# Two matmuls in place of three in the token-half products of a two-layer decoder trunk on one Trainium2 core

## The chip, the cores and the metric

The kernel runs on one core of a Trainium2 chip. The metric is the device time of one execution in microseconds. Three runs of the kernel before gave 1172.56, 1173.91 and 1175.39 us, so its median is 1173.91 us. One further execution was taken by the hardware profiler and took 1172.98 us; every duration quoted below comes from that one execution.

## The reference: what is computed

One sequence of 512 tokens with 1024 features passes through two layers in float32. Each layer is a token mixer, a layer norm over (alpha times the residual plus the mixer's output), a two-matrix feed-forward block of width 4096 with a squared ReLU, and a second layer norm:

```
mix = jnp.concatenate([s5_out, sb_out], axis=-1) @ mix_w_out[i] + mix_b_out[i]   # layer 0
mix = conformer_conv(x, ...)                                                     # layer 1
x = layer_norm(DEEPNORM_ALPHA * x + mix, ln1_g[layer], ln1_b[layer])
ffn = sqrelu_mlp(x, ffn_w1[layer], ffn_b1[layer], ffn_w2[layer], ffn_b2[layer])
x = layer_norm(DEEPNORM_ALPHA * x + ffn, ln2_g[layer], ln2_b[layer])
```

The mixer of layer 0 is a state-space part beside stick-breaking attention; that of layer 1 is a gated projection, a causal depthwise convolution of 31 taps, a layer norm, a swish and a projection.

## The kernel before, in words

Activations lie with features on the 128 partitions and the 512 tokens along the free dimension, in tiles of 128x512. Every operand of a large product is split into a high part (rounded to the matmul's input type) and a low part (the rest). ScalarE writes the high part and VectorE the low one, L246 and L247 for activations, L110 (`whi`) and L111 (`wlo`) for weights. `gemm` (L250) then spends three matmuls for each block of 128 features: high weights by high activations, high weights by low activations, low weights by high activations, all summed in one PSUM bank (L256). Each of the three loads its own 128x128 weights into TensorE.

**Tails.** Three products are followed by a layer norm and are therefore done in two token halves of 256 columns each, by the class `Tail` (L1004): tail "a", the attention half of layer 0's mixer output (4 feature blocks `cat[4:8]`, PSUM tiles `tla`); tail "b", the last feed-forward block of layer 0 (8 hidden blocks `hs`, tiles `tlb`); tail "d", the last projection of layer 1's convolution module (8 blocks `cs`, tiles `tld`). Each has 8 output tiles per half, 16 in all. When one is complete, VectorE adds it to the residual tile X (L389 with a bias in tails a and b, L385 without one in tail d), and adds X into a running sum over the 8 tiles (`sa`, `sb`, `sd`, L385).

**Layer norm and lead.** `tail_norm_lead` (L1058) sets the order. The first token half of the tail comes first. Then the norm of that half is interleaved with products of the second half: a matmul with a matrix of ones averages the running sum over the features (`mpa` and so on, L954), VectorE subtracts the mean from the 8 X tiles, ScalarE squares them, VectorE adds the squares in pairs, eight more matmuls average them (`vpa`), ScalarE and three small VectorE operations form the reciprocal square root (`ra`, `ta`), and for each of the 8 tiles VectorE scales X, ScalarE writes the new high part (`xah`) and VectorE the new low part (`xal`, L994). `BEFORE = (1, 3, 1, 2)` says how many products at least stand ahead of each averaging matmul. The next product, "lead" (class `Lead`, tiles `fl` and `pl`), uses the normed half at once, and while it works on the first half of the tokens the second half is normed.

**Order of the work.** A planner (the Tile framework's list scheduler) turns the traced instructions into one fixed queue per engine. Among instructions that its own cost model holds ready, it takes the one that was traced first. Each engine then works through its queue in order. In the convolution stage, TensorE, VectorE and ScalarE are kept in the order of `CONV_ORDER` by explicit dependencies (`in_order`); the first three products of tail d (the entries "t") lie inside that order. Weights are fetched and split ahead of use (`Weights._prep`, L85): when a tail in layer 0 asks for its weights, up to 5 further units are split too, and these are traced ahead of the tail's additions.

**Buffers.** Split activations lie in a pool of 24 pages of 128x512 (`page`, L208), and half of the hidden activations of the feed-forward blocks of layer 0 in 16 somewhat longer pages (`hpage`, L877), which the convolution uses later. Output tiles lie in 6 PSUM banks (`nps`, L871).

Of the kernel before, what the change touches and what calls it, by code (L numbers as in the profile page):

```python
# [10 lines left out]
F32R = mybir.dt.float32r  # L11
I32 = mybir.dt.int32
AF = mybir.ActivationFunctionType
ALU = mybir.AluOpType
PSUM = bass.MemoryType.PSUM

P = 128
T = 512
H = 256
D = 1024  # L20
KT = D // P
# [171 lines left out]
        self.run.append(ins.name)  # L193


@with_exitstack
def kernel(ctx: ExitStack, tc: tile.TileContext, a: dict, out: bass.AP):
    nc = tc.nc
# [6 lines left out]
    def const(shape, name, dt=F32):  # L205
        return cst.tile(shape, dt, tag=name, name=name)

    def page(name, dt=F32R):  # L208
        return pgp.tile([P, T], dt, tag="pg", name=name, bufs=24)

    X = [const([P, T], f"X{j}") for j in range(KT)]
    ident = const([P, P], "ident")
# [32 lines left out]
    def split(hi, lo, src):  # L245
        i0 = S.copy(hi, src).ins  # L246
        i1 = V.tensor_sub(lo, src, hi.bitcast(F32)).ins  # L247
        return i0.name, i1.name

    def gemm(ps, w, ksl, xs, c0, c1, start=True, stop=True):  # L250
# [6 lines left out]
                                stop=stop and k == n - 1 and i == 2).ins  # L257
        return ins


    wst = ExitStack()
    wpool = wst.enter_context(tc.tile_pool(name="mw", bufs=1))
# [68 lines left out]
    xs, w0, u0 = [], None, mm("u0")  # L331
# [11 lines left out]
    for j in range(KT):  # L343
        ps = (mm if j % 2 else s5ps)(f"xT{j}")
        for b in range(4):
            ins = PE.transpose(ps[:, b * P : (b + 1) * P], xin[j][:, b, :], ident).ins
            if j == 0 or j > 2:
                tc.add_manual_dep(ins, u0_last.name, NOSYNC, reason="order of the first products")
        xh, xl = page(f"x0h{j}"), page(f"x0l{j}")
# [6 lines left out]
        xs.append((xh, xl))  # L356
# [27 lines left out]
    def tt(o, x, y, op):  # L384
        V.tensor_tensor(o, x, y, op=op)  # L385
        return o

    def stt(o, x, s, y, op0, op1):
        V.scalar_tensor_tensor(o, x, s, y, op0=op0, op1=op1)  # L389
        return o  # L390
# [290 lines left out]
    def attention(p):  # L681
# [74 lines left out]
                              start=summed[h] == 1, stop=summed[h] == 4, skip_group_check=True)  # L756

        def closed(_):
            ch, cl = page(f"ch{p}"), page(f"cl{p}")
            split(ch, cl, made["av"])  # L760
            cat[4 + p] = (ch, cl)

        return {"t": turned, "s": scores, "w": weigh, "v": values, "e": closed}

# [5 lines left out]
    def gelu(q):  # L770
        g1 = spage(f"g1{q}")
        act(g1, vv[q], AF.Square)
        ts(g1, g1, GELU_A, 1.0, ALU.mult, ALU.add)
        tt(g1, g1, vv[q], ALU.mult)
        act(g1, g1, AF.Tanh, scale=GELU_C)
        stt(g1, g1, 1.0, vv[q], ALU.add, ALU.mult)
        for t in range(4):
            nc.sync.dma_start(Yd[q].rearrange("(r f) (t c) -> t f r c", r=4, t=4)[t], g1[32 * t : 32 * t + 32])
        yf = att.tile([P, T], F32, tag="wt", name=f"yf{q}", bufs=MIX_BUFS[4])
        nc.sync.dma_start(yf, Yd[q])  # L780
        yh, yl = page(f"yh{q}"), page(f"yl{q}")
        act(yh, yf, AF.Copy, scale=0.5)
        stt(yl, yf, 0.5, yh.bitcast(F32), ALU.mult, ALU.subtract)
        ys.append((yh, yl))

    glu_ws = []

    def glu(m):
        if m % 2 == 0:
            glu_ws[:] = W.next(), W.next()  # L790
        wv, wg = glu_ws
        sl = slice(m % 2 * P, (m % 2 + 1) * P)
        pg_, pv_ = mm(f"gg{m}"), mm(f"gv{m}")
        gemm(pg_, wg, sl, ys, 0, T)
        gemm(pv_, wv, sl, ys, 0, T)
        sg = spage(f"sg{m}").rearrange("p r c -> p (r c)")
# [4 lines left out]
        ch, cl = page(f"gh{m}"), page(f"gl{m}")  # L801
        split(ch, cl, o)
        cat[m] = (ch, cl)


    mo_w = []
# [56 lines left out]
    wp2 = wst.enter_context(tc.tile_pool(name="w2", bufs=1))  # L863
    hst = ExitStack()
    hid = hst.enter_context(tc.tile_pool(name="hid", bufs=1, side="right"))
    nps_ = ctx.enter_context(tc.tile_pool(name="nps", bufs=6, space=PSUM))
    sps_ = ctx.enter_context(tc.tile_pool(name="stp", bufs=2, space=PSUM))
    HALVES = ((0, H), (H, T))
# [5 lines left out]
    def stp(name):  # L874
        return sps_.tile([P, T], F32, tag="st", name=name)

    def hpage(name, dt=F32R, w=T):  # L877
        return hid.tile([P, PAD + T + 2], dt, tag="hid", name=name, bufs=16)[:, :w]
# [125 lines left out]
    class Tail:  # L1004
# [67 lines left out]
    def ffn1(layer, bi, k0, nb, xs, fps, first=()):  # L1072
        hs = []
        for i in range(nb):
            m = k0 + i
            if i < len(first):
                ps = first[i]
            else:
                ps = fps(f"f{layer}{m}")
                gemm(ps, W.next(), slice(0, P), xs, 0, T)  # L1080
            r = tmp(f"fr{layer}{m}")
            act(r, ps, AF.Relu, bias=pv("ffn_b1", 32 * layer + m))
            tt(r, r, r, ALU.mult)
            pg_ = page if (i < 4) == (bi % 2 == 0) else hpage
            hh, hl = pg_(f"hh{layer}{m}"), pg_(f"hl{layer}{m}")
            split(hh, hl, r)
            hs.append((hh, hl))
# [27 lines left out]
    for bi, nb in enumerate(FFN_BLOCKS[0]):  # L1115
# [390 lines left out]
```

## Time and profile before

| | before |
|---|---|
| median of three runs | 1173.91 us |
| profiled execution | 1172.98 us |
| its span (first to last instruction) | 1171.2 us |
| outside the span | 1.8 us |
| TensorE busy | 1138.9 us, 97% |
| VectorE busy | 822.9 us, 70% |
| ScalarE busy | 551.7 us, 47% |
| granted TensorE clock, mean | 0.993 |

PE is TensorE's matmul side, PEld its weight loads, DVE VectorE, ACT ScalarE. In a timeline each row has the start, the time until the last of its instructions ended, the engine, the line, the tiles as out<-in, the shape, how many instructions the row merges, and in brackets the idle time of the engine before it with what ended it. The last instructions of a merged row overlap: a row's time divided by its count is longer than the distance from start to start for short rows. In a table by stretches, each engine has its busy time and instruction count. Sums of times below are taken against the profiled execution of 1172.98 us.

### The profile page before, as it was taken

The page shows a single profiled execution, that of the slowest core. Times are in us where ns is not written, and L with a number is a line of the kernel's source. Part 1 is how long each engine was busy: PE and PEld are TensorE (multiplying, and loading weights), DVE is VectorE, ACT ScalarE, POOL GpSimd, SP SyncE. Part 2 cuts the span into 40 slices and gives each one's busy share as a digit, 9 for nine tenths or more (in the row PEclk, how much of TensorE's full clock was granted, in tenths as well). Part 3 has the DMA queues.
Part 4 walks back from the last instruction along what each step waited for, and adds up shares of the span by engine and source line. Part 5 has one row for each costly group of instructions (what it writes and reads, how often), then busy time and mean ns, then how long its engine had stood idle before and what let it go on. Part 6 is the DMA issues. An engine that isn't in the chain of part 4 may idle for free.

```text
span 1171.2 us, 17896 instructions
## 1 busy us (share of the span) xinstructions
PE 1138.9 (97%) x7180; PEld 953.1 (81%) x7180; DVE 822.9 (70%) x1396; ACT 551.7 (47%) x838; POOL 67.0 (6%) x125
## 2 busy tenths in 40 slices
PE   9989999999999999999999999899989999999997
PEld 7777767799888888888999777599968888887885
DVE  7999875498646546546555899886785958587337
ACT  7857779345425425425323132662753536363530
POOL 1022210000000000000021110001000000000000
PEclk9999999999999999999999999999989999999999
DMA  8521221332688788788454742206324151514211
GB/s 216 165 56 50 79 85 46 110 116 73 221 286 289 250 287 290 249 286 286 164 177 152 247 144 74 75 9 209 91 79 138 56 151 37 170 36 153 63 55 72
DMA packets 145907, 169.59 MB, mean 145 GB/s; under 512 B 13922, under 2 KB 119138, under 8 KB 145824
## 3 DMA queue, kind: packets, MB, share of 16 engines
q1 hardware_dynamic: 137024, 136.96, 36.7%
q0 software_dynamic: 8640, 31.46, 7.9%
q8 instruction: 56, 0.92, 0.3%
q14 instruction: 27, 0.22, 0.1%
q10 hardware_dynamic: 160, 0.03, 0.0%
HBM read 132.12 MB, written 35.65 MB: 143 GB/s over the span
## 4 chain that ended last, share of the span: by engine, by line
PE 82%; DVE 9%; ACT 4%; issue 2%; DMA 2%; POOL 0%; SPq 0%; DVEq 0%; ACTq 0%; POOLq 0%
PE f L256 24%; PE acf L256 11%; PE s L1390 8%; PE fl L256 5%; PE tlb L256 4%; PE tld L256 4%; PE h L1436 4%; PE pv L256 3%; PE pg L256 3%; PE cw L1165 3%; PE tla L256 2%; PE acmo L256 2%; PE pl L256 2%; DVE wlo L111 1%; PE gg L256 1%
## 5 line engine op out<-in xcount | busy, mean ns | idle before, releaser
L110 ACT CAST whi<-raw 128x1024 fp32r<-128x1024 f32 (+1 forms) x150 | 156.7, 1061 | 257.9 <-PE acf L256 61.0
L111 DVE TENSOR_TENSOR wlo<-raw,whi 128x1024 fp32r<-128x1024 f32 (+1 forms) x150 | 183.8, 1238 | 123.9 <-ACT whi L110 120.5
L256 PE MATMUL f<-xdh,whi 128*128 128x512 f32 x208 | 81.0, 390 | 1.0 <-ACT whi L110 1.0
L256 PE MATMUL f<-xah,whi 128*128 128x512 f32 x208 | 81.1, 390 | 0.0
L256 PE MATMUL f<-xal,whi 128*128 128x512 f32 x208 | 80.9, 389 | 0.0
L256 PE MATMUL f<-xah,wlo 128*128 128x512 f32 x208 | 80.9, 389 | 0.0
L256 PE MATMUL f<-xdl,whi 128*128 128x512 f32 x208 | 80.9, 389 | 0.0
L256 PE MATMUL f<-xdh,wlo 128*128 128x512 f32 x208 | 80.9, 389 | 0.0
L256 PE MATMUL acf<-hh,whi 128*128 128x512 f32 x192 | 75.4, 392 | 0.0
L256 PE MATMUL acf<-hh,wlo 128*128 128x512 f32 x192 | 75.2, 392 | 0.0
L256 PE MATMUL acf<-hl,whi 128*128 128x512 f32 x192 | 74.8, 390 | 0.0
L1390 PE MATMUL s<-whi,ah 128*128 128x512 f32 x168 | 66.0, 400 | 3.3 <-ACT whi L110 2.5
L1390 PE MATMUL s<-wlo,ah 128*128 128x512 f32 x168 | 66.4, 402 | 2.3 <-DVE wlo L111 2.3
L1390 PE MATMUL s<-whi,al 128*128 128x512 f32 x168 | 66.0, 396 | 0.0
L111 DVE TENSOR_TENSOR wlo<-quad,whi 128x1536 fp32r<-128x1536 f32 x28 | 49.0, 1754 | 4.7 <-ACT whi L110 4.4
L110 ACT CAST whi<-quad 128x1536 fp32r<-128x1536 f32 x28 | 41.0, 1478 | 21.9 <-PE f L256 8.0
L389 DVE SCALAR_TENSOR_TENSOR cy<-hp,wdw,cy 128x512 f32<-128x512 f32 (+1 forms) x75 | 49.5, 660 | 0.2 <-ACT cy L185 0.2
L95 POOL DMA_DIRECT2D whi<-kepth x30 | 16.1, 536 | 547.7 <-PE tlb L256 385.5
L256 PEld LDWEIGHTS f<-xdh,whi 128*128 128x128 f32 x208 | 39.0, 188 | 9.4 <-ACT whi L110 1.4
L256 PEld LDWEIGHTS f<-xah,whi 128*128 128x128 f32 x208 | 39.0, 188 | 8.2
L256 PEld LDWEIGHTS f<-xdh,wlo 128*128 128x128 f32 x208 | 39.0, 188 | 8.2
L256 PEld LDWEIGHTS f<-xah,wlo 128*128 128x128 f32 x208 | 39.0, 188 | 8.1
(649 smaller groups left out, 3069.1 us busy)
## 6 DMA issues: line engine op xcount, KB each, us to landing
raw<-in_ffn_w_dram SPq DMA_DIRECT2D x35, 1024.0 KB, 5.6
kepth<-whi SPq DMA_DIRECT2D x30, 512.0 KB, 3.4
keptl<-wlo SPq DMA_DIRECT2D x30, 512.0 KB, 9.4
whi<-kepth POOLq DMA_DIRECT2D x30, 512.0 KB, 3.6
wlo<-keptl POOLq DMA_DIRECT2D x30, 512.0 KB, 4.6
raw<-in_ffn_w_dram SPq DMA_DIRECT2D x28, 512.0 KB, 4.1
raw<-in_conv_w_pw_dram SPq DMA_DIRECT2D x12, 1024.0 KB, 7.3
quad<-in_ffn_w_dram SPq DMA_DIRECT2D x16, 768.0 KB, 4.8
```

What stands on the lines that cost most here:

```text
L95: nc.gpsimd.dma_start(x, d)
L110: i0 = nc.scalar.copy(hi, raw).ins
L111: i1 = nc.vector.tensor_sub(lo, raw, hi.bitcast(F32)).ins
L256: ins = PE.matmul(ps[:, c0:c1], u[:, k, ksl], v[:, c0:c1], start=start and k == 0 and i == 0, stop=stop and k == n - 1 and i == 2).ins
L389: V.scalar_tensor_tensor(o, x, s, y, op0=op0, op1=op1)
L1165: PE.matmul(cps[j, c0][g][C, :], Ds[j][t // 16][R, t % 16, :], hps[j][R, t + c0 : t + c1], start=t < 4, stop=t >= n - 4, tile_position=(R. ...
L1390: PE.matmul(ps, u, v[:, p, :], start=chain == i and p == 0 and n_ == 0, stop=p == len(As) - 1 and n_ == 2, skip_group_check=True)
L1436: PE.matmul(ps, u, v, start=k == 0 and i == 0, stop=k == nb_last - 1 and i == 2)
```

## The change

For the tails alone, `gemm` gives way to `side_by_side`. The high and low parts of one activation block now lie side by side in one tile of 128x2x512 (a `Twin`). One matmul takes the high weights once and streams 256 columns of the high and 256 columns of the low part, 512 in all, into a whole PSUM bank; a second matmul takes the low weights and streams the 256 columns of the high part into the bank's first half. The bank's second half therefore holds high weights by low activations, and VectorE adds it to X with an operation of its own ahead of the one that was there. All other products keep `gemm`. So that the parts lie side by side, the page pool becomes 12 tiles of two pages; single pages are handed out as halves of such a tile. The 16 longer pages are replaced, in the feed-forward stage, by 8 tiles of two pages in a pool of their own, and the longer pages open in its place when tail b has been traced.

```diff
+class Twin(tuple):
+    def __new__(cls, t):
+        self = super().__new__(cls, (t[:, 0, :T], t[:, 1, :T]))
+        self.both = t[:, :, :T]
+        return self
...
+    spare = []
+    def twin(name):
+        return Twin(pgp.tile([P, 2, T], F32R, tag="pg", name=name, bufs=12))
     def page(name, dt=F32R):
-        return pgp.tile([P, T], dt, tag="pg", name=name, bufs=24)
+        if not spare:
+            t_ = pgp.tile([P, 2, T], dt, tag="pg", name=name, bufs=12)
+            spare[:] = t_[:, 1], t_[:, 0]
+        return spare.pop()
...
+    def side_by_side(ps, w, ksl, xs, c0, c1):
+        for k, x in enumerate(xs):
+            PE.matmul(ps, w[0][:, k, ksl], x.both[:, :, c0:c1], start=k == 0, stop=k == len(xs) - 1, skip_group_check=True)
+            ins = PE.matmul(ps[:, :H], w[1][:, k, ksl], x[0][:, c0:c1], start=False, stop=k == len(xs) - 1, skip_group_check=True).ins
+        return ins
...
+    hst2 = ExitStack()
+    htw = hst2.enter_context(tc.tile_pool(name="htw", bufs=1, side="right"))
+    hpg = []
...
     def new_x(name):
-        return [(page(f"{name}h{j}"), page(f"{name}l{j}")) for j in range(KT)]
+        return [twin(f"{name}{j}") for j in range(KT)]
...
-                last = gemm(ps, self.ws[j // nj], slice((j % nj) * P, (j % nj + 1) * P), self.xk, c0, c1)
+                last = side_by_side(ps, self.ws[j // nj], slice((j % nj) * P, (j % nj + 1) * P), self.xk, c0, c1)
                 x = X[j][:, c0:c1]
+                tt(x, ps[:, H:], x, ALU.add)
                 if self.bias is None:
-                    tt(x, ps[:, c0:c1], x, ALU.add)
+                    tt(x, ps[:, :H], x, ALU.add)
                 else:
-                    stt(x, ps[:, c0:c1], self.bias[:, j : j + 1], x, ALU.add, ALU.add)
+                    stt(x, ps[:, :H], self.bias[:, j : j + 1], x, ALU.add, ALU.add)
...
     xs, first = tail_norm_lead(hs, "b", rb[1], ("ln2_g", 0), ("ln2_b", 0), 4, "pl")
+    hst2.close()
+    hpg.append(hst.enter_context(tc.tile_pool(name="hpg", bufs=1, side="right", reuse_waits="tile")))
```

The other places of the diff only build twins where two pages stood (x0, y, g, c, the hidden tiles).

More of the change, by code (lines that the diff above doesn't have):

```diff
@@ L348 @@
                 tc.add_manual_dep(ins, u0_last.name, NOSYNC, reason="order of the first products")
-        xh, xl = page(f"x0h{j}"), page(f"x0l{j}")
+        xh, xl = x0 = twin(f"x0{j}")
         with tc.high_priority():
@@ L355 @@
         S.copy(X[j], ps)
-        xs.append((xh, xl))
+        xs.append(x0)
         if j > 1:
@@ L758, in closed @@
         def closed(_):
-            ch, cl = page(f"ch{p}"), page(f"cl{p}")
-            split(ch, cl, made["av"])
-            cat[4 + p] = (ch, cl)
+            cat[4 + p] = twin(f"c{p}")
+            split(*cat[4 + p], made["av"])
         return {"t": turned, "s": scores, "w": weigh, "v": values, "e": closed}
@@ L780, in gelu @@
         nc.sync.dma_start(yf, Yd[q])
-        yh, yl = page(f"yh{q}"), page(f"yl{q}")
+        yh, yl = y = twin(f"y{q}")
         act(yh, yf, AF.Copy, scale=0.5)
         stt(yl, yf, 0.5, yh.bitcast(F32), ALU.mult, ALU.subtract)
-        ys.append((yh, yl))
+        ys.append(y)
     glu_ws = []
@@ L800, in glu @@
         V.tensor_copy(o.rearrange("p (c t) -> p t c", t=4), sg.rearrange("p (t c) -> p t c", t=4))
-        ch, cl = page(f"gh{m}"), page(f"gl{m}")
-        split(ch, cl, o)
-        cat[m] = (ch, cl)
+        cat[m] = twin(f"g{m}")
+        split(*cat[m], o)
     mo_w = []
@@ L875, in stp, with htwin @@
         return sps_.tile([P, T], F32, tag="st", name=name)
+    def htwin(name):
+        return Twin(htw.tile([P, 2, T], F32R, tag="hid", name=name, bufs=8))
     def hpage(name, dt=F32R, w=T):
-        return hid.tile([P, PAD + T + 2], dt, tag="hid", name=name, bufs=16)[:, :w]
+        return hpg[0].tile([P, PAD + T + 2], dt, tag="hid", name=name, bufs=16)[:, :w]
     def tmp(name, dt=F32):
@@ L1083, in ffn1 @@
             tt(r, r, r, ALU.mult)
[L1084 to L1087, printed above, removed]
+            hs.append((twin if (i < 4) == (bi % 2 == 0) else htwin)(f"h{layer}{m}"))
+            split(*hs[-1], r)
             for k in keep_at.get(("f", m), ()) if layer == 0 else ():
```

## The prediction, as put on record

> **What bounds the kernel now.** I read the page's busy times first, then the chain of work that ended last.
>
> ```profile
> span 1171.2 us, 17896 instructions
> PE 1138.9 (97%) x7180; PEld 953.1 (81%) x7180; DVE 822.9 (70%) x1396; ACT 551.7 (47%) x838; POOL 67.0 (6%) x125
> PE 82%; DVE 9%; ACT 4%; issue 2%; DMA 2%; POOL 0%; SPq 0%; DVEq 0%; ACTq 0%; POOLq 0%
> ```
>
> TensorE is the bound overall. But a mean of 70% for VectorE says nothing about a stage, so I asked for busy times by stretches, with the end of tail a and its norm in the first four and tails b and d in the last two:
>
> ```profile
> 234.00:240.00 6.00, 5.93 (x49) 5.96 (x50) 5.47 (x7) 2.84 (x3) 0.00 (x0) 1.00 0.56 171
> 240.00:250.00 10.00, 10.00 (x83) 9.85 (x82) 9.32 (x21) 3.18 (x4) 0.00 (x0) 1.00 0.76 240
> 250.00:260.00 10.00, 10.00 (x79) 9.79 (x79) 9.84 (x26) 4.59 (x13) 0.00 (x0) 1.00 0.02 5
> 260.00:267.00 7.00, 7.00 (x60) 7.00 (x60) 6.36 (x17) 2.32 (x5) 0.00 (x0) 1.00 0.00 0
> ...
> 566.00:619.00 53.00, 53.00 (x417) 51.66 (x416) 31.28 (x67) 13.16 (x25) 7.57 (x14) 1.00 0.48 163
> 758.00:811.00 53.00, 52.85 (x420) 50.86 (x417) 41.81 (x112) 26.45 (x58) 6.34 (x12) 1.00 0.36 120
> ```
>
> Columns after the length are PE, PEld, DVE, ACT, POOL. In tail a TensorE and VectorE are both full: 9.84 of 10 us at 250 to 260. In tail b VectorE is busy 31.28 of 53 us, in tail d 41.81 of 53. The same change meets three different stages.
>
> **What TensorE saves.** Counts are from the views of the tiles, pitches from the chain in order of time, where a run of like matmuls is one row:
>
> ```profile
> L256 PE MATMUL tla<-ch,whi x64: 278/283/466, 234.1 to 259.1; 128*128 128x256 f32 x64
> L256 PE MATMUL tlb<-hh,whi x128: 277/283/471, 571.0 to 618.7; 128*128 128x256 f32 x128
> L256 PE MATMUL tld<-csh,whi x128: 279/283/467, 758.1 to 810.2; 128*128 128x256 f32 x128
> ```
> ```profile
> 439.91 43.52 PE f L256 x192
> ...
> 788.86 8.63 PE tld L256 x72
> ```
>
> 512 columns take 43.52/192 = 226.7 ns from start to start, 256 columns 8.63/72 = 119.9 ns. The 256 further columns cost 106.8 ns, so each matmul carries 13.1 ns that do not depend on its columns. Three matmuls of 256 are 359.7 ns, one of 512 plus one of 256 is 346.6: 13.1 ns saved per block and output tile. That is 64 x 13.1 = 0.84 us in tail a and 128 x 13.1 = 1.68 us each in tails b and d, 4.2 us in all. No row shows a matmul whose moving columns come in two pieces, or the two widths alternating. Bounds: nothing saved, or all fixed parts hidden (39.3 ns, 12.6 us); I take 13.1 ns, since both widths pay the same fixed part in these rows. The Trainium skill ("TensorE: Matmul & The Clock Gate", section Back-to-back issue gap) gives N/2.4 + 2.5 ns, thus a fixed part of only 2.5 ns; the rows show five times that. By the Trainium skill's page, as an estimate, the three tails together would save 0.8 us, and the sum below would be +3.6 us instead.
>
> **What VectorE pays.** 16 additions per tail, 48 in all, of the form in tail d's row:
>
> ```profile
> L385 DVE TENSOR_TENSOR X<-tld,X x16: 409/420/426, 763.5 to 810.8; 128x256 f32<-128x256 f32 x16
> ```
>
> Queued behind an independent instruction, such an operation moves the queue by less than its duration. Tail a's VectorE timeline:
>
> ```profile
> 237.21 0.48 DVE L389 SCALAR_TENSOR_TENSOR X<-tla,rb,X 128x256 f32<-128x256 f32 x1 [0.53 <-PE tla L256]
> 237.61 2.35 DVE L111 TENSOR_TENSOR wlo<-raw,whi 128x1024 fp32r<-128x1024 f32 x2
> ...
> 246.70 0.88 DVE L385 TENSOR_TENSOR sa<-sa,X 128x256 f32<-128x256 f32 x2
> ...
> 248.36 1.75 DVE L385 TENSOR_TENSOR X<-X,mpa 128x256 f32<-128x256 f32 x5 [0.40 <-PE mpa L954]
> ...
> 255.60 0.42 DVE L389 SCALAR_TENSOR_TENSOR ta<-vpa,ra 128x256 f32<-128x256 f32 x1
> ...
> 257.66 1.27 DVE L389 SCALAR_TENSOR_TENSOR X<-X,PV,ra 128x256 f32<-128x256 f32 x3
> ...
> 267.54 2.74 DVE L385 TENSOR_TENSOR X<-X,mpa 128x256 f32<-128x256 f32 x8 [1.14 <-PE mpa L954]
> ```
>
> Five independent ones take 1.75 us: (1.75 - 0.42)/4 = 0.33 us each. Two of which the second needs the first take 0.88: 0.46 us. The new addition and the old one write the same X, so 0.46 holds unless the planner puts something between them. Bounds 0.33 and 0.46; I take 0.33, because in a full stage the planner has other work to put between.
>
> *Tail a.* Before the first mean come 8 new additions, 2.7 us, of which the 0.53 us idle ahead of 237.21 takes part: the mean is 2.1 us late. The ninth tile's addition fits the 0.40 us of idle at 248.36. Those of tiles 10 to 12 are traced ahead of `ta`, another 1.0 us. So the first new high part is D = 3.1 us late. What waits is TensorE's lead:
>
> ```profile
> 258.18 1.32 ACT L185 ACTIVATE xah<-X,PV 128x256 fp32r<-128x256 f32 x3 [2.71 <-DVE X L389]
> ```
> ```profile
> 259.46 0.40 PE L256 MATMUL fl<-xah,whi 128*128 128x256 f32 x2
> ```
> ```profile
> 276.00 0.56 PE L256 MATMUL fl<-xah,whi 128*128 128x256 f32 x3
> 276.59 0.39 PE L256 MATMUL fl<-xal,whi 128*128 128x256 f32 x1
> ```
>
> The first high part is there at 258.18 + 0.5 = 258.7, the lead starts at 259.46: 0.8 us of slack. With D = 3.1 the lead starts 2.3 us late, although the tail's matmuls end 0.84 us earlier. For the second half, tiles 13 to 16 add 1.3 us, so its norm is 4.4 us late in all. There the slack is some 0.2 us: TensorE has run out of first-half products by 276.00, where it picks up the second half's first high parts and then waits 0.3 us. So tail a ends in a loss of 4.4 - 0.2 = 4.2 us; its saving of 0.84 is spent as waiting. Bounds: -0.84 us (all hidden) and 16 x 0.46 - 0.53 - 0.2 = +6.6 us. From there on the stage is TensorE's again: 165 x 0.1199 = 19.8 us of matmuls fill 20.17 us, so the loss stays.
>
> ```profile
> 276.59 20.17 PE fl L256 x165
> ```
>
> *Tail b.* The additions hide: TensorE's places for the averaging matmuls are set by the products ahead of them, not by VectorE.
>
> ```profile
> 600.24 1.43 DVE L385 TENSOR_TENSOR sqb<-sqb,sqb 128x256 f32<-128x256 f32 x4
> ...
> 616.42 0.48 DVE L994 SCALAR_TENSOR_TENSOR xbl<-X,PV,xbh 128x256 fp32r<-128x256 f32 x1
> ...
> 619.79 0.42 DVE L385 TENSOR_TENSOR sb<-sb,X 128x256 f32<-128x256 f32 x1
> ```
> ```profile
> 606.10 1.73 PE vpb L954 x8
> ...
> 619.23 2.88 PE pl L256 x24
> ```
>
> The squares are summed at 601.7, the matmul that needs them starts at 606; the last low part is ready at 616.9, the lead starts at 619.23; the second half's sum is ready at 620.2, its mean stands behind one lead product of 2.88 us that started at 619.23. Each has over 1.5 us to spare against 0.46 us per addition. I take 1.6 of the 1.68 us, and if that cover were gone, up to 16 x 0.46 = 7.4 us could show.
>
> *Tail d.* VectorE keeps a fixed order there, and the first product waits for the low parts, the ninth for those of the second half:
>
> ```profile
> 761.53 0.43 DVE L247 TENSOR_TENSOR csl<-cy,csh 128x256 fp32r<-128x256 f32 x1 [0.52 <-ACT csh L246]
> ...
> 786.90 0.43 DVE L247 TENSOR_TENSOR csl<-cy,csh 128x256 fp32r<-128x256 f32 x1 [0.42 <-ACT csh L246]
> ```
>
> The first product loses its 0.1 us of gain. The low part at 786.90 comes later by up to four additions, 1.3 us, and only the ninth product's last block needs it; TensorE has seven other blocks of the next products to do meanwhile. I take 1.5 us of 1.68.
>
> *Pages and pools.* Every user of a page takes them in pairs already, so the buffers come free at the same times: nothing. The two `D` tiles and one memset that VectorE does at 555.76 may have to wait until tail b, at 619, frees the hidden tiles under the new longer pages. `D` is first needed at 666.6, and VectorE is busy for only 8.63 + 4.26 of the 25 us from 620 on. Cost 0 to 1.0 us, taken as 0.
>
> ```profile
> 620.00:635.00 15.00, 14.86 (x115) 14.39 (x114) 8.63 (x24) 5.96 (x14) 0.47 (x1) 1.00 0.27 91
> 635.00:645.00 10.00, 10.00 (x85) 10.00 (x84) 4.26 (x11) 2.75 (x6) 3.18 (x6) 1.00 0.46 145
> ```
> ```profile
> 555.76 1.02 DVE L1173 TENSOR_TENSOR D<-mask,wdw 128x512 f32<-128x512 f32 x2
> ```
> ```profile
> L1165 PEld LDWEIGHTS cw<-hp,D x1224: 101/103/106, 666.6 to 757.0; 32*32 32x32 f32 x175
> ```
>
> **Sum.** +4.2 - 1.6 - 1.5 = +1.1 us on the profiled 1172.98 us, thus 1174.1. That execution was 0.9 us below the median of the runs; carried over to the median, 1173.91 + 1.1 = 1175.0 us. Within 0.2% (2.3 us) is about what a measurement of this kernel cannot tell from no change.
>
> **Rivals.** *A second price in tail a (slower).* If additions cost 0.46 us each, tail a loses 6.6 us, and TensorE idles for 12 x 0.46 - 0.53 - 0.8 + 0.84 = 5 us ahead of the lead. An idle stretch lowered the clock once here:
>
> ```profile
> 851.00:854.00 3.00, 0.85 (x6) 0.42 (x5) 1.74 (x3) 3.00 (x5) 0.00 (x0) 1.00 0.00 0
> 854.00:858.00 4.00, 3.43 (x10) 2.44 (x9) 3.42 (x3) 3.26 (x5) 0.00 (x0) 0.64 0.00 0
> ```
>
> 2.15 us without a matmul in 3, then a granted clock of 0.64 over 4 us: 4 x 0.36 = 1.4 us lost. Sum 6.6 + 1.4 - 3.1 = +4.9: 1178.8 us. The result turns slower as soon as tail a loses more than the 3.1 us that b and d gain. For it: the two additions are dependent; against: the planner's habit of filling. The Trainium skill ("TensorE: Matmul & The Clock Gate", section Why this matters for your kernels) advises against gaps of over some 3 us between bursts; the stretch here was shorter and already cost clock. *Hidden in tail a (faster).* Weights are split up to five units ahead, so of the `wlo` operations in that stretch, such as the two at 237.61, most are for the lead and are not needed until 259; if the planner moves two of them (2.35 us) and later ones behind the additions, all gains show: -0.84 - 1.6 - 1.5 = -3.9, 1170.0 us. Against: they are traced first, and the two at 237.61 go ahead of additions that follow. *The side-by-side matmul saves nothing*, because two-piece columns or the alternation cost as much as the fixed part: +4.2, 1178.1 us. The Trainium skill's fixed part of 2.5 ns ("TensorE: Matmul & The Clock Gate", section Back-to-back issue gap) would come close to this case. *The views are held to overlap*: if the planner takes a twin's half-token view for one range, products 5 to 8 of tail d wait for the second half's low parts, some 6 us: 1181 us.
>
> **Chances.** Forecast 0.48 (own range 1172.6 to 1177.4, from +-2.4 us for tail a): 0.03 faster, 0.35 same, 0.10 slower. Second price 0.17, all slower. Hidden 0.25: 0.21 faster, 0.04 same. No saving 0.05 and overlap 0.05, slower. Together faster 0.24, same 0.39, slower 0.37. The range, 1169.4 to 1179.4, takes in most of the hidden case and of the second price.
>
> **What would show it.** Right: tail rows of 512 and 256 columns with about 347 ns per pair; a stretch after tail a in which TensorE waits for `xah`, VectorE still full; tails b and d shorter by 1.5 us with no new wait. Wrong: no wait ahead of the lead; pairs of 360 ns or more; a wait for `csl` in tail d's fifth product; a granted clock under 1 at 255 to 265.

## The result, and the profile after

The changed kernel takes 1179.14 us (median of 20 runs, 1174.87 to 1182.09), the kernel before took 1175.20 us beside it (20 runs, 1169.41 to 1178.28). The ratio is 1.0035, 95% interval 1.0026 to 1.0045: some 4 us slower, three to five. The forecast was 1175.0 us, a loss of 1.1 us, with 1169.4 to 1179.4 as the range; the measured time lies in it, 0.3 us below its upper edge.

The page of the changed kernel's profiled execution (1178.2 us) begins with

```profile
span 1176.5 us, 17329 instructions
PE 1140.5 (97%) x6860; PEld 939.3 (80%) x6860; DVE 836.8 (71%) x1444; ACT 551.3 (47%) x838; POOL 66.4 (6%) x125
PE 70%; DVE 13%; ACT 4%; issue 2%; DMA 1%; POOL 0%; SPq 0%; DVEq 0%; ACTq 0%
```

320 matmuls fewer, 48 operations of VectorE more, as the change says. In the chain that ended last, TensorE falls from 82% to 70% and VectorE rises from 9% to 13%. The stretches of tail a, and then of tails b and d, stand in the same view as before (columns after the length: PE, PEld, DVE, ACT, POOL):

```profile
235.00:241.00 6.00, 6.00 (x35) 5.26 (x36) 5.96 (x9) 2.73 (x3) 0.00 (x0) 1.00 0.60 181
241.00:251.00 10.00, 10.00 (x60) 8.74 (x59) 8.90 (x19) 3.05 (x3) 0.00 (x0) 1.00 0.72 239
251.00:261.00 10.00, 9.01 (x48) 7.29 (x46) 9.94 (x29) 3.27 (x9) 0.00 (x0) 1.00 0.00 0
261.00:268.00 7.00, 4.84 (x27) 4.70 (x28) 7.00 (x20) 3.27 (x8) 0.00 (x0) 0.76 0.01 4
572.00:625.00 53.00, 53.00 (x293) 45.88 (x292) 36.77 (x82) 13.32 (x25) 7.60 (x14) 1.00 0.49 167
764.00:817.00 53.00, 52.41 (x302) 44.22 (x301) 46.78 (x128) 26.87 (x58) 6.32 (x12) 1.00 0.35 120
```

At the end of tail a VectorE is full (9.94 of 10, then 7.00 of 7 us) and TensorE, full before, now stands idle: 9.01 of 10, then 4.84 of 7 us. Tails b and d stay TensorE's. Dividing the two traces by the first matmul of each stage gives, in us (lengths worked out from the starts, differences before rounding; the lead counts to its tail):

```
                                     before    after   difference
start to tail a                      234.07   235.00     +0.93
tail a, lead, to FFN layer 0          62.52    67.01     +4.49
FFN layer 0                          274.41   275.44     +1.02
tail b, to second half of its lead    62.84    62.06     -0.77
convolution                          124.24   125.18     +0.94
tail d, lead, to the residual         89.18    88.14     -1.04
rest                                 323.99   323.66     -0.32
```

The change touches the second, third, fourth and sixth of these: +4.49 + 1.02 - 0.77 - 1.04 = +3.70 us, within the measured three to five. The first row differs between executions of kernels whose queues there are equal (+1.95 us in one of the experiments, +5.79 in another). The convolution has new tiles too, but its +0.94 cannot be told from such differences: it lies between -0.51 and +2.56 us in the experiments, and is +1.39 in an execution of e5 below, which has the old code there. So only the four stages are compared below.

In tail a the chain in order of time, and the waits of TensorE, show what sets the end:

```profile
262.60 0.52 ACT xa L185
263.12 0.04 issue
263.16 9.59 PE fl L273 x65
...
281.06 0.52 ACT xa L185
281.58 0.04 issue
281.63 20.55 PE fl L273 x168
```
```profile
PE fl L273 <- ACT xa L185: 3.1, 1, 3.1
PE tla L280 <- DVE X L412: 0.9, 1, 0.9
```

The 3.1 us are new: the lead stands ready and waits for the first high part, which VectorE's norm lets through late. Before, only the row of 0.9 us was there. The granted clock answers that idle stretch. In windows around it,

```profile
259.80:263.16 3.36, 0.25 (x2) 0.00 (x1) 3.36 (x10) 0.56 (x2) 0.00 (x0) 0.95 0.00 0
262.84:266.26 3.42, 3.10 (x14) 2.96 (x14) 3.42 (x10) 2.35 (x6) 0.00 (x0) 0.50 0.02 5
```

0.25 us of matmuls in 3.36 are followed by 3.42 us at half clock. By the Trainium skill ("TensorE: Matmul & The Clock Gate", section What's actually happening) the clock falls to half after an idle window of some 3.4 us and returns after a busy one of that length; the trace agrees, though the 3.36 us were not wholly idle.

### The profile page after: what moved, and what is told of

Its sections match the earlier page's. It is cut to its first block, busy times and chain, and to the rows that moved or that the text cites. A ratio compares the mean times of both kernels' runs of the same rounds, so it can differ in the third digit from the quotient of the medians.

```text
span 1176.5 us, 17329 instructions
## 1 busy us (share of the span) xinstructions
PE 1140.5 (97%) x6860; PEld 939.3 (80%) x6860; DVE 836.8 (71%) x1444; ACT 551.3 (47%) x838; POOL 66.4 (6%) x125
## 4 chain that ended last, share of the span: by engine, by line
PE 70%; DVE 13%; ACT 4%; issue 2%; DMA 1%; POOL 0%; SPq 0%; DVEq 0%; ACTq 0%
PE f L273 22%; PE acf L273 11%; PE s L1418 8%; PE fl L273 5%; PE h L1464 4%; DVE cy L412 3%; DVE cz L412 3%; PE tlb L280 3%; PE tld L280 2%; PE acmo L273 2%; PE pl L273 2%; PE tlb L281 1%; DVE wlo L111 1%; DVE X L408 1%; PE tld L281 1%
## 5 line engine op out<-in xcount | busy, mean ns | idle before, releaser
L273 PE MATMUL f<-xd,whi 128*128 128x512 f32 x416 | 128.2, 389 | 1.0 <-ACT whi L110 1.0
L273 PE MATMUL f<-xa,whi 128*128 128x512 f32 x416 | 128.3, 389 | 0.0
L273 PE MATMUL acf<-h,whi 128*128 128x512 f32 x384 | 120.0, 394 | 0.0
L273 PEld LDWEIGHTS f<-xd,whi 128*128 128x128 f32 x416 | 78.0, 188 | 17.6 <-ACT whi L110 1.4
L273 PEld LDWEIGHTS f<-xa,whi 128*128 128x128 f32 x416 | 77.9, 188 | 16.1
L273 PEld LDWEIGHTS acf<-h,whi 128*128 128x128 f32 x384 | 72.1, 188 | 16.6
L273 PE MATMUL f<-xa,wlo 128*128 128x512 f32 x208 | 80.9, 389 | 0.0
L273 PE MATMUL f<-xd,wlo 128*128 128x512 f32 x208 | 80.9, 389 | 0.0
L273 PE MATMUL acf<-h,wlo 128*128 128x512 f32 x192 | 75.3, 392 | 0.0
L280 PE MATMUL tld<-cs,whi 128*128 128x512 f32 x128 | 45.7, 399 | 0.5 <-DVE cs L264 0.5
```

Of the source, the lines that this page charges most:

```text
L273: ins = PE.matmul(ps[:, c0:c1], u[:, k, ksl], v[:, c0:c1], start=start and k == 0 and i == 0, stop=stop and k == n - 1 and i == 2).ins
L280: PE.matmul(ps, w[0][:, k, ksl], x.both[:, :, c0:c1], start=k == 0, stop=k == len(xs) - 1, skip_group_check=True)
```

## The experiments

Columns: difference of a stage to the kernel before in one profiled execution each, in us; then the timed ratio to the kernel before with its 95% interval.

```
                       tail a   FFN 0   tail b   tail d   ratio
after                   +4.49   +1.02    -0.77    -1.04   1.0035 (1.0026 to 1.0045)
e1_buffers              +0.06   +1.09    +0.62    -0.28   1.0003 (0.9983 to 1.0023)
e2_b_d                  -0.17   +1.91    -0.76    -0.72   0.9989 (0.9971 to 1.0007)
e3_a_alone              +4.82   +1.51    -0.01    -0.47   1.0056 (1.0034 to 1.0077)
e4_a_no_add              0.00   +1.01    -0.52    -0.48   1.0010 (0.9993 to 1.0027)
e5_before_plus_adds     +4.23   +1.40    -0.08    -0.11   1.0038 (1.0020 to 1.0057)
e6_two_ahead            +7.91   +1.01    -0.78    -1.31   1.0063 (1.0041 to 1.0085)
e7_pool                 +7.29   +1.29    -0.37    -1.26   1.0050 (1.0026 to 1.0074)
e8_grouped              +0.07   +1.00    -0.91    -0.30   0.9987 (0.9975 to 0.9999)
```

**Which part of the change costs.** The theory: VectorE's additions in tail a cost 4.5 us, the buffers 1.0, tails b and d give 0.75 and 1.04 back. The rival: the loss is spread over many small things. Three kernels take the parts singly. In `Tail.run` the products and the additions go by the tail's name (cut at the three dots):

```diff
-                last = side_by_side(ps, self.ws[j // nj], ...)
+                pair_ = self.ln.n in "bd"      # "-" in e1, "a" in e3
+                last = (side_by_side if pair_ else gemm)(ps, self.ws[j // nj], ...)
+                o = ps[:, :H] if pair_ else ps[:, c0:c1]
-                tt(x, ps[:, H:], x, ALU.add)
+                if pair_:
+                    tt(x, ps[:, H:], x, ALU.add)
```

> The new kernel with its twin pages and its two pools of hidden tiles, but with the old 24 matmuls of 256 columns per block set and the single old addition in all three tails. Nothing of the computation is left out. Theory: the buffers alone cost 1.0 us in FFN layer 0, because the matmuls that read hidden tiles in their new place have a longer pitch (231.0 ns in the block mean where it was 228.9), and nothing elsewhere: +1.0 to +1.5 us against the kernel before, tails a, b and d as long as before within 0.4 us. Rival (the prediction's zero for pages and pools): 0.0 us, and the 1.0 us in FFN layer 0 comes from something else that tail a set off.

> The new kernel with the old products and the old single addition in tail a; tails b and d side by side as in the new kernel. Nothing of the computation is left out. Theory (tail a loses 4.5 us, b and d gain 0.75 and 1.04, buffers cost 1.0): tail a and its lead as long as before within 0.4 us, no wait of TensorE ahead of the lead of over 1 us, and in all -0.8 us against the kernel before (between -1.5 and 0). Rival (the loss of 4 us is spread over clock windows and buffers and does not hang on tail a): +2 us or more.

> The new kernel with the products side by side and the second addition in tail a alone; tails b and d with the old products. Nothing of the computation is left out. Theory: tail a +4.5 us, buffers +1.0, no gains in b and d, so +5.5 us against the kernel before, and the start of the lead's first product 2.8 us later within tail a, as in the new kernel. Rival (spread): less than +3 us.

The stages come out as the theory said: tail a +0.06 and -0.17 with old products there, +4.82 with new ones, and FFN layer 0 is at least 1.0 us longer in all three, whichever tail is changed. What it has beyond 1.0 are single long steps of up to 0.73 us from one matmul to the next, where the last hidden tile of a block comes late. So the buffers alone carry the 1.0 us, and tail a alone the rest. In all, by the timed ratios, e1 +0.4, e2 -1.3 and e3 +6.6 us; e1's own interval (-2.0 to +2.7 us) cannot tell its theory from its rival, the stage does. e1's +0.62 in tail b contains a single step of 0.90 us from one matmul to the next that e3, with the same products there, does not have (-0.01).

**VectorE's additions or TensorE's products?** Two kernels cut between them: e4 keeps the new products and leaves out the 16 additions in tail a, e5 keeps the old products and adds 16 additions that nobody needs.

```diff
+                if pair_ and self.ln.n not in "a":     # e4, with pair_ in all three tails
                     tt(x, ps[:, H:], x, ALU.add)
```
```diff
                 x = X[j][:, c0:c1]                     # e5, in the kernel before
+                if self.ln.n == "a":
+                    tt(hpage(f"dump{c0}{j}", F32)[:, c0:c1], ps[:, c0:c1], x, ALU.add)
```

> The new kernel without the 16 new additions in tail a: there the product of the high weights with the low activations is computed on TensorE but left out of the sum. Theory (it is VectorE's 16 additions that make tail a late): tail a's lead starts 0.3 to 0.8 us earlier than before, not 2.8 us later; with the buffers' 1.0 us and the gains of b and d the whole is -1.6 us against the kernel before (between -2.5 and -0.8). Rival (the two-piece matmul itself or the bank's two halves read in turn makes tail a late): +3 us or more, with the wait ahead of the lead still there.

> The kernel before, with 16 further additions of 128 x 256 on VectorE in tail a, each into a tile that nobody reads; products, buffers and tails b and d as before, nothing left out. Theory (16 additions of 0.33 us on a full VectorE are the whole price in tail a): first high part 3.1 to 3.5 us later and the lead's first product 2.3 to 2.8 us later than before within tail a, tail a to the end of its lead +4.2 to +4.7 us, elsewhere 0, so +4.5 us in all. Rival (the two-piece product, or the bank's two halves, makes tail a late): under +1 us.

TensorE's waits in tail a and its lead, of e4 and then of e5:

```profile
PE tla L280 <- ACT whi L110: 0.9, 1, 0.9
```
```profile
PE fl L256 <- ACT xah L185: 2.4, 1, 2.4
PE tla L256 <- DVE X L389: 0.9, 1, 0.9
```

Without the additions the wait ahead of the lead is gone and the stage is as long as before (0.00); with the additions alone, at old products, it is there with 2.4 us and the stage is 4.23 us longer. The additions are the price. e5 missed in FFN layer 0, where 0 was expected and +1.40 came with the old buffers: 0.8 us are single long steps in one block, where a hidden tile came late, and the rest a longer pitch of the products from hidden tiles (233.1 ns in the mean, 231.2 before). Its unread tiles come out of the pool of the hidden tiles, so these may lie in other places of it; their places were not read. e4 missed in one thing: its lead starts 0.42 us earlier within the stage, but the stage ends where it ended before. In the chains of e4 and of the kernel before, the lead's first matmuls:

```profile
264.61 0.62 PE fl L273 x3
265.23 0.02 issue
265.26 7.49 PE fl L273 x60
```
```profile
259.63 7.44 PE fl L256 x62
```

63 matmuls take 8.1 us in e4 where 62 took 7.4. Four of e4's first steps are 0.19 to 0.30 us instead of 0.12: the lead has caught up with the norm and takes its parts as they come. VectorE's last sum ahead of the second mean ends 32.6 us into the stage, 32.3 before. So TensorE's saving in tail a has no place to come out, with the additions or without. e4 was expected at -1.6 us in all; its timed +1.2 us has an interval from -0.8 to +3.2, and its touched stages sum to 0.0.

**Order or total?** If what hurts is that the low parts of the lead's weights stand ahead of the additions on VectorE, preparing two units ahead instead of five mends it (e6). If it is VectorE's load, giving four of these subtractions to GpSimd mends it (e7).

```diff
+        ahead, W.ahead = W.ahead, 2 if name == "a" else W.ahead      # e6, tail_norm_lead
         t = Tail(xk, ln, bias)
...
+        W.ahead = ahead
```
```diff
-                i1 = nc.vector.tensor_sub(lo, raw, ...)               # e7, Weights._prep
+                i1 = (nc.gpsimd if self.done in self.other else nc.vector).tensor_sub(lo, raw, ...)
...
+    W.other = range(W.done + 2, W.done + 6)
```

> The new kernel, with weights prepared two units ahead instead of five while tail a and its lead run; nothing left out. Three low parts of the lead's weights (3 x 1.18 us on VectorE) then stand behind the first half's norm. Theory (the order on VectorE is the price: work that is not yet needed stands ahead of the additions): tail a to the end of its lead within 1 us of before, so -1 us in all against the kernel before (between -2 and 0). Rival (VectorE's total is the price, and what is moved is owed before the lead ends): tail a still +3 us or more, and waits of the lead's later products for the moved low parts.

> The new kernel, with four low parts of the lead's weights subtracted on GpSimd instead of VectorE in tail a; nothing left out. VectorE has 4.7 us less to do ahead of the first norm. Theory (VectorE's load ahead of the norm is the price): tail a to the end of its lead within 0.5 us of before, -1 us in all against the kernel before. Rival (GpSimd is too slow for it or slows VectorE while both read): tail a still +2 us or more.

Both theories fell and both rivals stood. e6's lead starts on time (0.61 us earlier within the stage than before), and then pays twice, as its waits of TensorE show:

```profile
PE fl L273 <- ACT xa L185: 3.2, 2, 3.0
PE fl L273 <- DVE wlo L111: 2.7, 1, 2.7
```

The second half's first high part comes 43.5 us into the stage: 2.6 us earlier than in the changed kernel, but still 2.2 later than before, so the lead, which started on time, runs out of work. Behind it the lead waits 2.7 us more for a low part that was put off. The order only chooses which product waits. In e7 the low parts take GpSimd 2.4 to 2.6 us each, VectorE 1.22, and while GpSimd works VectorE's own sums (`sa`) take four to six times as long (timelines of GpSimd and VectorE):

```profile
242.06 4.93 POOL L111 TENSOR_TENSOR wlo<-raw,whi 128x1024 fp32r<-128x1024 f32 x2 [10.41 <-ACT whi L110]
247.91 4.94 POOL L111 TENSOR_TENSOR wlo<-raw,whi 128x1024 fp32r<-128x1024 f32 x2 [0.92 <-ACT whi L110]
```
```profile
245.17 2.11 DVE L408 TENSOR_TENSOR sa<-sa,X 128x256 f32<-128x256 f32 x1
247.20 0.41 DVE L408 TENSOR_TENSOR X<-tla,X 128x256 f32<-128x256 f32 x1
...
248.17 2.42 DVE L408 TENSOR_TENSOR sa<-sa,X 128x256 f32<-128x256 f32 x1
250.51 0.41 DVE L408 TENSOR_TENSOR X<-tla,X 128x256 f32<-128x256 f32 x1
```

The sums with two operands in SBUF stall until GpSimd's instruction is done, the additions with one operand in PSUM (0.41 us) do not. The Trainium skill ("GPSIMD Engine Reference", section 1. Specifications) says that GpSimd shares SBUF interfaces with VectorE and that an instruction with two SBUF inputs contends; the trace agrees.

**What the buffers cost, and why b and d gain half.** Four kernels of matmuls alone measure the pitch. The first has a row of equal matmuls for each width, and 24 of 512 columns from each second of 94 pages; the second repeats the accumulating products of FFN layer 0 at the very addresses of the two kernels. Each of the four was run once.

> Not the trunk: a kernel of matmuls alone, with nothing else running, and with none of the reference's computation. 24 matmuls of 512 columns are read from each second of 94 pages of 2 kB that fill most of the SBUF from low to high addresses, then runs of 96 of 512 columns, of 256, of two pieces of 256, and of pairs of 512 and 256, once from low pages and once from high ones. Theory (the place of the moving operand sets its pitch): low pages 226.5 to 227 ns from start to start, the pages of the upper tenth 230 ns and more. Rival (the longer pitch of hidden tiles comes from the other engines' traffic or from the change of weight slots): all pages within 0.5 ns. Pairs: the side-by-side form in low pages 347 ns (prediction), by a fixed part that does not shrink 360.

> Again matmuls alone and none of the reference's computation. The first accumulating products of FFN layer 0 are repeated with the moving and stationary operands at the very addresses that they have in the kernel before (pa) and after (pb), 192 matmuls of 512 columns each, with no other engine at work; then with the weights 96 kB lower (pc), with the hidden tiles of the upper pool alone (pd), with the pages alone (pe), and once more with VectorE and ScalarE busy on other tiles (ph). Theory (two operands in the upper part of the SBUF get in each other's way): pa about 229, pb 231, pd 231 or more, pe and pc 226.7 ns; ph as pa. Rival (traffic of the other engines): all 226.7 but ph 229 or more. Then pairs side by side: eight of 512 columns and eight of 256 after them (pf) against 512 and 256 in turn (pg). Theory (a change of width costs some 7 ns per pair): pf 346.6 ns per pair, pg 353.9. Rival (the two pieces or the weights cost it): pf as pg.

From the chains in order of time of the first and the second (start, us, tile, count):

```profile
263.15 21.76 PE pac L92 x96
284.91 11.51 PE pad L96 x96
```
```profile
76.37 44.35 PE pb L84 x192
120.72 43.97 PE pc L84 x192
164.69 44.23 PE pd L84 x192
208.92 43.53 PE pe L84 x192
252.45 33.49 PE pf L84 x192
285.95 33.94 PE pg L84 x192
```

Equal widths take 21.76/96 = 226.7 and 11.51/96 = 119.9 ns, as in the kernel. But 512 and 256 in turn (pg, 96 pairs) take 33.94/96 = 353.5 ns, not 346.6; eight of the one and then eight of the other (pf) 348.9. So here the change of width costs most of what the shorter count saves: against three of 256 (359.7 ns) the pair saves 6 ns, not 13. In the first kernel the pairs took 353.3 ns from start to start with two pieces as well as with 512 columns in a row, so the two pieces cost nothing.

The trunk itself does not always pay this. In the changed kernel's timeline, 18 pairs of tail a lie between these two rows:

```profile
240.62 0.39 PE L280 MATMUL tla<-c,whi 128*128 128x512 f32 x1
...
246.86 0.39 PE L280 MATMUL tla<-c,whi 128*128 128x512 f32 x1
```

That is 6.24/18 = 346.7 ns, the forecast. Worked out from the starts, for output tiles that no averaging matmul and no wait interrupts, in ns per block:

```
                                   before          after
tail a                             358.8 to 360.0  346.5 to 346.8
tail b                             355.4 to 356.8  349.5 to 351.9
tail d, 6th to 12th product        360.0           346.6 to 346.8
tail d, 14th to 16th product       360.0           352.4 to 353.9
```

So the same alternation costs nothing in one place and some 7 ns a pair in another. What sets this is open: the matmuls alone, all with operands at equal remainders (below), gave the longer value only.

The buffers' loss is in the same rows. pb, with the new kernel's addresses and nothing else at work, takes 44.35 us, to the hundredth what the new kernel takes; the kernel before had 43.95 (chains of after, then of before):

```profile
313.08 44.35 PE acf L273 x192
...
446.19 43.52 PE f L273 x192
```
```profile
307.66 43.95 PE acf L256 x192
```

So traffic is out as a cause of the longer pitch: ph, with VectorE and ScalarE busy, was as pc without them (229.0 ns a matmul both). pe, the pages alone, takes 226.7 ns, pd, the hidden tiles alone, 230.4. My theory, that the upper part of the SBUF is slow, was already at odds with the first kernel, where all pages up to 213 kB but the first one read took 226.7 ns. The third and the fourth kernel look for what it is instead.

> Matmuls of 512 columns alone, none of the reference's computation. pa: the hidden tiles' sequence of the kernel before, moved 100 kB down; pb: the pages' sequence, moved 140 kB up; pc: each hidden place 12 times running; pd: the hidden places in rising order; pe: the hidden sequence's weights with one hidden place for all; pf: hidden places with the pages' weights; pg: pages with the hidden tiles' weights; ph: three operands in turn (first, second, first) at ten offsets. Theory (the region above 176 kB is slow): pb, pc, pd, pe, pf 230 ns and more, pa and pg 226.7. Rival (it is the weights' places that go with them): pa, pe and pg slow, pb and pf 226.7. Second rival (the order of places, or their spacing, whatever the region): pa, pd and pf slow, pb, pc, pe and pg 226.7.

> Matmuls of 512 columns alone, none of the reference's computation: eight places of the weights (pa to ph: 18 kB in a tile of their own, then 27, 41, 66, 98, 135, 164 and 201 kB) by twelve places of the moving operand (27 to 211 kB, in rising order), 16 matmuls for each pair. Theory (the pair of places counts: the first study of places had its weights at 18 kB and was fast everywhere, the third at 135 kB and was slow from 94 kB up): pa 226.7 for all twelve; pf 226.7 up to 71 kB and 229 to 235 from 90 kB up; the other rows show where the border goes with the weights. Rival (something else than the places told the two studies apart): pa slow from 90 kB up as pf, or pf fast everywhere.

```profile
41.79 22.19 PE pa L84 x96
63.97 22.39 PE pb L84 x96
...
130.71 21.98 PE pe L84 x96
152.69 22.11 PE pf L84 x96
174.80 21.76 PE pg L84 x96
```

In the third kernel the hidden sequence 100 kB lower stays slow (pa, 22.19/96 = 231.1), the pages' sequence 140 kB higher becomes slow (pb, 233.2), and pages with the other weights stay fast (pg, 226.7): neither the region theory, which wanted pa fast, nor the rivals fit. The fourth settles it. The mean pitch of ten steps, in ns, worked out from the starts, by the address of the weights (three of eight rows) and of the moving operand; below each address its remainder by 256:

```
moving       26752  40608  55296  71328  90112 106496 122880 139264 155648 180352 194688 211072
mod 256        128    160      0    160      0      0      0      0      0    128    128    128
weights
 18560 (128) 226.6  233.5  233.2  233.5  233.2  232.2  231.7  233.0  233.1  229.2  226.7  226.6
 65536 (0)   233.3  234.6  226.7  234.3  226.7  226.7  226.6  226.7  226.7  233.3  233.3  233.4
134816 (160) 233.3  226.6  233.9  228.8  233.9  233.1  233.2  233.7  233.1  233.0  233.3  233.3
```

Where both start at the same remainder, the matmul takes 226.7 ns; where they do not, 231.7 to 234.6 (229.2 and 228.8 stand right behind unequal pairs, and the pitch takes up to some ten matmuls to settle). The other five rows, all with weights at remainder 0, 128, agree. The period is 256 B: in the third kernel an operand with the weights' remainder by 128 but not by 256 was slow (232.2 ns). In pc of the second kernel, with the weights moved by 375 x 256 B, the sequence kept its pitch (229.0). The rule tells which rows above take 226.7 ns and which take longer, though not how much longer (pe of the third kernel, unequal, took 229.0): the first kernel had all its operands at 128; in the trunk, by the addresses that the second kernel repeats, the weights and pages lie at 160, the old hidden pages, 2176 B apart, at 224 and 96, the new twins at 128. By it the trace's own 512-column matmuls divide: those of FFN layer 0's first products, which read pages, take 226.7 ns in both kernels; the accumulating ones from hidden tiles 231.2 ns before and 233.5 after. 287 of these by 2.3 ns make 0.7 of the 1.0 us, and the pages read right behind them, which settle more slowly (227.4 before, 228.6 after), 0.3. A kernel with the twins moved to the weights' remainder was not run, so that it heals the trunk is argued, not shown.

**A version that uses this.** e8 takes the products side by side in b and d alone, all 512-column products of a tile ahead of its 256-column ones, and sets the twins' halves 2176 B apart.

```diff
         for k, x in enumerate(xs):
             PE.matmul(ps, w[0][:, k, ksl], x.both[:, :, c0:c1], ...)
+        for k, x in enumerate(xs):
             ins = PE.matmul(ps[:, :H], w[1][:, k, ksl], x[0][:, c0:c1], ...)
```

> As the kernel with side-by-side products in tails b and d alone, but with the 512-column products of all blocks of a tile ahead of its 256-column ones instead of in turn, and with the hidden twins' two halves 2176 B apart, as in the kernel before. Nothing left out. Theory (a change of width costs TensorE; by the matmuls alone 349.5 ns a pair in groups of eight, 354.0 in turn): tails b and d 0.6 us shorter each than with pairs in turn, so -1.3 each against before, FFN layer 0 +0.2 to +1.0 by the twins' new place, tail a 0; in all -1.5 to -2.4 us by the stages. Rival (grouping brings nothing in the kernel, or the later 256-column products delay VectorE): b and d -0.8 each or worse.

The timed ratio is 0.9987 (0.9975 to 0.9999): 1.5 us faster than before, at the edge of what this can tell, and not to be told from e2 (0.9989). The stages don't bear the theory out: they sum to -0.1 us instead of -1.5 to -2.4, with tail b -0.91 instead of -1.3, and tail d -0.30, less than in turn. By the undisturbed tiles grouping gains nothing in the trunk: 351.6 to 351.8 ns a pair in tail b, and in tail d 349.1 to 349.2 throughout, between the two values of pairs in turn. And in tail d TensorE waits 1.3 us for the convolution's low parts,

```profile
PE tld L280 <- DVE cs L264: 1.3, 3, 0.4
```

where it waited 0.5 in the changed kernel: the three waits lie ahead of the sixth, seventh and eighth wide matmul of the first product, which ask for the low parts sooner than pairs do. FFN layer 0 stays at +1.00, but not for the same reason: two of its accumulating blocks take 44.16 us (43.95 and 44.18 before, 44.37 and 44.36 after), and the first one has 0.6 us in single steps, where a hidden tile came late. The longer pitch costs some 0.4 us here, with twins whose halves have remainders 128 and 0, neither of them 160.

## Why the prediction was right and wrong

- *Tail a.* Right in mechanism, near in size: 4.49 us lost, 4.2 forecast, with the lead 2.77 us late (2.3 forecast) and a new wait for the high part, VectorE full. The price of 0.33 us per addition held where another instruction stands between the two that write one X: two additions in a row take 0.75 us, so the second moves the queue by 0.33. Only in the first tile do the two stand next to each other (237.09 and 237.54 us, 0.45 apart). The first high part is 3.5 us late, not 3.1, and that this is so near is partly luck. Counted from the starts, 13 additions stand ahead of it, not 12, and take 4.6 us of the queue. VectorE's idle time up to there is 1.2 us where it was 1.4, so the 0.9 us of idle that the forecast set against the additions were not used: it now waits for `whi` in the rows below. But its other operations come out 0.9 us shorter, chiefly the sums (`sa`): one of them now stands behind the first high part, and the others no longer stand right behind the one they need.

```profile
240.21 0.75 DVE L408 TENSOR_TENSOR X<-tla,X 128x256 f32<-128x256 f32 x2
...
243.80 2.36 DVE L111 TENSOR_TENSOR wlo<-raw,whi 128x1024 fp32r<-128x1024 f32 x2 [0.66 <-ACT whi L110]
...
250.11 1.23 DVE L111 TENSOR_TENSOR wlo<-raw,whi 128x1024 fp32r<-128x1024 f32 x1 [0.44 <-ACT whi L110]
```

- *The lower bound of tail a, -0.84 us, was wrong*, and with it the rival "hidden in tail a" (-3.9 us): e4 shows 0.00 with no additions at all, since the earlier lead only catches up with the norm, and e6 shows that moving work behind the additions costs more than it gives.
- *"13.1 ns saved per block and output tile" held in some places and failed in others.* The fixed part is right for equal widths, and tail a's pairs take the 347 ns that were named as a sign of being right, but there the saving had no place to come out. Products 6 to 12 of tail d take as little; in its last three the alternation eats half of the saving. For tail b the forecast carried over tail d's 119.9 ns a matmul, where the trace had 118.9 (8.56/72, row below, from the chain before): three of 256 took 356.7 ns there, not 359.7, and the pairs take 351, so 5 to 6 ns are saved per block, 128 x 5.5 = 0.7 us. There -0.52 to -0.78 came out in four of five kernels with pairs in turn; in tail d those with pairs have -0.48 to -1.31 against -0.11 to -0.47 without. No pair of an undisturbed tile took 360 ns in the changed kernel, so the rival "saves nothing" fell. The Trainium skill's 2.5 ns ("TensorE: Matmul & The Clock Gate", section Back-to-back issue gap) would have given 0.3 us per tail of 128 blocks; the measured 5 to 13 ns decide.

```profile
597.54 8.56 PE tlb L256 x72
```

- *Additions hidden in b and d: right.* TensorE is busy 53.00 of 53 us in tail b with VectorE at 36.77, and tail d has no wait in its fifth product, so the twins' views were not held to overlap.
- *"Pages and pools: nothing" failed*, by 1.0 us in FFN layer 0. The forecast asked when buffers come free; what changed was where they lie. The `D` tiles that might have waited for tail b cost nothing that shows.
- *The rival of a second price* was wrong in its price (0.33, not 0.46) and right that the idle stretch costs clock: 3.4 us at half. That adds little to the loss. 14 matmuls of the lead take some 0.21 us each instead of 0.12, 1.3 us in all; but the second mean, which starts behind the lead's first 65 matmuls at 272.59, could not have started before VectorE's last sum at 272.15 (below), so at most 0.4 us of the 4.49 are the clock's.

```profile
271.72 0.43 DVE L408 TENSOR_TENSOR sa<-sa,X 128x256 f32<-128x256 f32 x1
```

- *The sum.* +4.2 - 1.6 - 1.5 = +1.1 was forecast, +4.49 - 0.77 - 1.04 + 1.02 = +3.70 came. Tail a, the doubtful term, was off by 0.3; the two gains that seemed safe were off by 1.3 together, the zero by 1.0. The time passed the range of the forecast alone (to 1177.4 us) and stayed within the wide one.

## What to carry to other kernels

Work moved from an engine that is idle on average to one that is full in this stage is paid in full there: look at the stage, then give the change only to the stages where the receiving engine has room, as e2 and e8 do (their gains show in the stages; in the whole time they are at or within the noise). A saving of a few nanoseconds per matmul must be measured in the very sequence of widths and places in which it is to come. And when tiles are allocated anew, compare their addresses, not only their lifetimes.

## What the runs showed of the hardware that was not expected

- A 512-column fp32r matmul takes 226.7 ns from start to start if weights and moving operand start at the same remainder by 256 B in the partition, some 229 to 235 ns if not, with nothing else at work (one execution per kernel). The region of the SBUF and the other engines' traffic made no difference.
- 512 and 256 columns in turn take 353.3 to 353.5 ns a pair in matmuls alone, 7 more than the two widths take among their own kind. In the trunk they take 346.5 to 353.9 ns, by the place; why is open.
- While GpSimd subtracts 128 x 1024 (2.4 to 2.6 us), a VectorE sum of 128 x 256 from two SBUF operands takes up to 2.42 us instead of 0.42, and one with a PSUM operand still 0.41.
